# The first conditioning product of a two-layer streaming encoder, taken in two halves of its columns

## The chip, the cores and the metric

The kernel runs on one core of a Trainium2 chip. Five engines of that core matter here: TensorE (PE) for matmuls and transposes, VectorE (DVE) and ScalarE (ACT) for elementwise work and for emptying PSUM, GpSimd (POOL) for a few small things, and SyncE (SP), whose queue issues every DMA of this kernel. Each engine runs its own instruction queue in order; semaphores tie them together. The metric is the device time of one execution in microseconds (us). Before the change the median of three runs is 2450.26 us (2447.16 to 2452.15).

## What is computed

The reference is one step of a two-layer encoder over 1024 prompt tokens and 32 sample tokens with 1024 features. Layer 0 is an mLSTM (a chunked matrix-memory mixer with four heads), layer 1 a band attention, and each is followed by a squared-ReLU MLP. What matters for the change is how the first layer's input is made:

```python
def ada_mod(c, w, b):
    return jax.nn.silu(c) @ w + b

sh1, sc1, g1, sh2, sc2, g2 = jnp.split(ada_mod(c, p['w_ada'][l], p['b_ada'][l])[:, None, :], 6, axis=-1)
u = x * (1 + sc1) + sh1
proj = u @ w_in                      # queries and keys, values v, output gate, input and forget gates
```

The vector c is one per sequence (prompt and sample). Shift sh1 and scale sc1 of layer 0 are the first two of six column blocks of w_ada, each 1024 wide: 1024 x 2048 numbers in float32, 8 MB. Nothing of layer 0 can start on u before them. All is float32, and the results must agree with the reference to float32 accuracy, so the large products are made of a high and a low part: each weight and each u is split in two float32r numbers, and three matmuls (high x high, high x low, low x high) make one.

## The kernel before, in words

Features lie on the 128 partitions in eight chunks (KC = 8); tokens are the free dimension, in three blocks TBS of 384, 384 and 288 (the last holds 256 prompt and the 32 sample tokens). A block of 384 is three tiles of 128 tokens.

The start runs like this. `ada_load(k)` fetches the first 2048 columns of w_ada for the 128 rows of chunk k as two loads of 512 KB into a tile `rada` of 8 KB per partition. These tiles come from the ring with the tag `wc`, six buffers that they share with split weights (`w_v`, `w_qk`) and with the rows of the second token block. `ada_mm(k)` multiplies silu(c) (in `cs`) with them, four matmuls of 512 columns into four groups of 32 partitions of one PSUM bank, added up over k. `ada_first` copies the bank to SBUF, transposes it in four pieces and adds the bias `pt2`; the result `ada` holds shift and scale with features on partitions.

Meanwhile `x_load` brings rows of x, and `x_transpose` turns each chunk over on TensorE (three transposes into a bank `xps`, one copy into `xt` by ACT or DVE). `u_chunks` makes u from `xt` and `ada`, chunk by chunk, as a high part (`modulate`: one ACT instruction) and a low part (two DVE instructions by way of `utmp`). `v_weight` loads half of the weights of the values of head 0 (`raw_v`, with 8 columns for the gates) and splits it (ACT makes the high part, DVE the low): w_v_0 covers the chunks 0 to 3, w_v_1 the chunks 4 to 7.

`v_first` then walks over the blocks: for each chunk k, for each token tile of the block, three matmuls of 264 columns (`v_chunk`), and after each chunk it calls `next_u`, which transposes x and makes u of the next block. In all 3 blocks, 9 token tiles, 8 chunks and 3 products are 216 matmuls. Then come the xsp stores of xt, the gate rows (`gate_rows`: transposes `gt`, then rows `ig`, `fr`, and scans on four partitions that end in the transposes `ae_ps`), queries and keys of the heads (`qk_proj`, weights `raw_qk` and `w_qk`), the mLSTM, the output gate, and from some 440 us on the MLP and layer 1. The conditioning for the other blocks of w_ada is made on DVE as filler work, from loads into `ada_room`.

The order in which instructions stand in each engine's queue isn't that of the source alone: a scheduler places them after a time model of its own, and it also decides which DMA stands where in SP's queue. A change at one place thus moves instructions behind it. `flow` is a list of generators that are advanced by `tick` from the main loops; at the start it holds only `small_params` (small loads of parameters).

## Time and profile before

| what | value |
|---|---|
| median of three runs | 2450.26 us |
| the profiled execution | 2451.64 us |
| its span, first to last instruction | 2449.7 us |
| TensorE busy, share of the span | 2386.9 us, 97% |
| VectorE busy | 1919.8 us, 78% |
| ScalarE busy | 1090.7 us, 45% |
| bytes moved, mean rate | 335.15 MB, 137 GB/s |
| mean granted TensorE clock | 0.993 |

Times in a profile row are microseconds from the start of the span. A row of the timeline has the start, the time taken, the engine (PEld is TensorE loading weights, SPq is SyncE's queue issuing DMAs), the line of the kernel, the operation, output and inputs by the program's names, the shape, the count, and in brackets how long the engine had been idle and what ended that. In a row of stretches the first two numbers are the stretch and its length; then comes the busy time and the count for each engine, the granted TensorE clock, the mean busy share of the 16 DMA engines (just above 1 where transfers overlap) and GB/s. A float32 matmul counts as two instructions there in the conditioning.

### The profile page before, as it was taken

How to read it: one execution, taken by the hardware profiler on the slowest of the kernel's cores; microseconds unless marked ns; L12 is line 12 of the kernel's file. 1: busy time of each engine (PE TensorE's matmuls, PEld its weight loads, DVE VectorE, ACT ScalarE, POOL GpSimd, SP SyncE). 2: the span in 40 equal slices, each digit the busy share in tenths (PEclk: the TensorE clock that was granted, in tenths of full speed). 3: DMA queues.
4: the chain of work that ended last, by engine and by line, in shares of the span. 5: the costliest groups of instructions: out<-in, count | busy, mean ns of one | idle time of the engine just before them, and what ended most of it. 6: DMA issues, size and time to landing. Idle time of an engine off the chain costs nothing.

```text
span 2449.7 us, 42910 instructions
## 1 busy us (share of the span) xinstructions
PE 2386.9 (97%) x16580; PEld 2294.7 (94%) x16580; DVE 1919.8 (78%) x4340; ACT 1090.7 (45%) x2264; POOL 167.3 (7%) x315
## 2 busy tenths in 40 slices
PE   7999999999999999999999999999999999899997
PEld 4999999999999999999999977789999999899997
DVE  4899998788678678687488666755998888887878
ACT  4554456283212212212157466763776777222212
POOL 0211100000000000000000224420000000000003
PEclk9999999999999999999999999999999999999999
DMA  7432223412233233233223230041486779966642
GB/s 287 137 102 88 89 80 109 157 35 87 89 101 121 87 104 113 82 116 107 89 77 101 64 73 2 10 117 42 159 275 233 255 256 335 376 234 230 228 156 72
DMA packets 251503, 335.15 MB, mean 137 GB/s; under 512 B 12824, under 2 KB 201644, under 8 KB 250276
## 3 DMA queue, kind: packets, MB, share of 16 engines
q1 hardware_dynamic: 251300, 332.42, 41.4%
q8 instruction: 130, 2.13, 0.4%
q14 instruction: 73, 0.60, 0.1%
HBM read 255.50 MB, written 79.24 MB: 137 GB/s over the span
## 4 chain that ended last, share of the span: by engine, by line
PE 76%; DVE 12%; DMA 4%; ACT 3%; issue 2%; POOL 0%; SPq 0%; ACTq 0%; DVEq 0%; POOLq 0%
PE dn L1409 11%; PE up L1300 6%; PE up L118 6%; PE up L120 6%; PE up L119 6%; PE dn L119 5%; PE dn L118 5%; PE dn L120 5%; PE pv L1749 3%; PE s L1692 2%; PE pt L1727 2%; PE o L118 1%; PE o L119 1%; PE o L120 1%; DMA hd<-HL 1%
## 5 line engine op out<-in xcount | busy, mean ns | idle before, releaser
L1409 PE MATMUL dn<-fx,wf_d 128*128 128x264 f32 x2016 | 254.2, 285 | 6.9 <-DVE ACX L986 3.3
L1409 PEld LDWEIGHTS dn<-fx,wf_d 128*128 128x128 f32 x2016 | 248.7, 188 | 9.3 <-issue 2.9
L119 PE MATMUL dn<-h,w_dn 128*128 128x384 f32 (+1 forms) x768 | 249.5, 325 | 0.0
L118 PE MATMUL up<-U,w_up 128*128 128x384 f32 (+1 forms) x768 | 249.2, 324 | 0.0
L119 PE MATMUL up<-U,w_up 128*128 128x384 f32 (+1 forms) x768 | 247.9, 323 | 0.0
L118 PE MATMUL dn<-h,w_dn 128*128 128x384 f32 (+1 forms) x768 | 247.8, 323 | 0.0
L120 PE MATMUL up<-U,w_up 128*128 128x384 f32 (+1 forms) x768 | 247.6, 322 | 0.0
L120 PE MATMUL dn<-h,w_dn 128*128 128x384 f32 (+1 forms) x768 | 247.3, 322 | 0.0
L986 DVE SCALAR_TENSOR_TENSOR ACX<-dn,ada,ACX 128x264 f32<-128x264 f32 (+5 forms) x400 | 160.1, 426 | 52.6 <-PE dn L1409 39.6
L238 DVE SCALAR_TENSOR_TENSOR aacc<-rada,cs,aacc 128x256 f32<-128x256 f32 x448 | 190.1, 476 | 0.0
L986 DVE SCALAR_TENSOR_TENSOR acc<-dn,ada,acc 128x384 f32<-128x384 f32 (+2 forms) x256 | 119.2, 485 | 47.0 <-PE dn L120 45.6
L1025 ACT ACTIVATE r<-up 128x384 f32<-128x384 f32 (+1 forms) x96 | 44.3, 463 | 243.3 <-PE up L120 236.9
L119 PEld LDWEIGHTS dn<-h,w_dn 128*128 128x128 f32 x768 | 144.5, 188 | 0.2 <-DVE h L1028 0.2
L120 PEld LDWEIGHTS dn<-h,w_dn 128*128 128x128 f32 x768 | 144.5, 188 | 0.0
L120 PEld LDWEIGHTS up<-U,w_up 128*128 128x128 f32 x768 | 144.3, 188 | 0.0
L118 PEld LDWEIGHTS up<-U,w_up 128*128 128x128 f32 x768 | 144.2, 188 | 0.1
L119 PEld LDWEIGHTS up<-U,w_up 128*128 128x128 f32 x768 | 144.2, 188 | 0.0
L118 PEld LDWEIGHTS dn<-h,w_dn 128*128 128x128 f32 x768 | 143.9, 187 | 0.2
L1300 PE MATMUL up<-u,wf_u 128*128 128x264 f32 x1056 | 139.6, 284 | 1.3 <-ACT wf_u L89 0.6
L1300 PEld LDWEIGHTS up<-u,wf_u 128*128 128x128 f32 x1056 | 132.6, 188 | 1.9 <-ACT wf_u L89 0.8
L1027 DVE TENSOR_TENSOR r<-r 128x384 f32<-128x384 f32 (+1 forms) x96 | 49.9, 522 | 103.3 <-ACT h L1026 102.9
L89 ACT CAST w_up<-raw_up 128x1024 fp32r<-128x1024 f32 x52 | 54.3, 1046 | 136.4 <-DMA raw_up<-in_w_up_dram 102.5
(386 smaller groups left out, 6575.0 us busy)
## 6 DMA issues: line engine op xcount, KB each, us to landing
rada<-in_w_ada_dram SPq DMA_DIRECT2D x64, 512.0 KB
hd<-HL SPq DMA_DIRECT2D x28, 1056.0 KB
raw_up<-in_w_up_dram SPq DMA_DIRECT2D x52, 512.0 KB
fx<-hd SPq DMA_DIRECT2D x50, 528.0 KB
hd<-HM SPq DMA_DIRECT2D x28, 792.0 KB
raw_dn<-in_w_down_dram SPq DMA_DIRECT2D x36, 512.0 KB
ada_room<-in_w_ada_dram SPq DMA_DIRECT2D x32, 512.0 KB
rdn_u<-in_w_up_dram SPq DMA_DIRECT2D x32, 512.0 KB
```

The lines of the kernel that those rows point to most:

```text
L89: nc.scalar.copy(dst_h, src)
L118: nc.tensor.matmul(ps, wh, mov(0, k), start=(k == 0), stop=False)
L119: nc.tensor.matmul(ps, wh, mov(1, k), start=False, stop=False)
L120: nc.tensor.matmul(ps, wl, mov(0, k), start=False, stop=(k == nk - 1))
L238: nc.vector.scalar_tensor_tensor(acc[:, cnd], raw[:, k], sc, acc[:, cnd], op0=ALU.mult, op1=ALU.add)
L986: nc.vector.scalar_tensor_tensor(xs, ps[:, off + o:off + o + mm_], gate[:, fc, cnd:cnd + 1], xs, op0=ALU.mult, op1=ALU.add)
L1027: nc.vector.tensor_mul(r, r, r)
L1300: nc.tensor.matmul(p, self.ws[w][:, wl, k], moving(f, tp, xl, k), start=first and k + n_ == 0, stop=k == 3 and n_ == 2, skip_group_check=n ...
L1409: nc.tensor.matmul(p, ws[w][:, wl, k], t[:, s0, xl], start=first and k + n_ == 0, stop=k == kg - 1 and n_ == 2, skip_group_check=not first)
L1692: nc.tensor.matmul(s[:, b, :w], qst, kk[i][:, g, k0 + j0:k0 + j0 + w], start=(i == 0), stop=(i == 1))
L1727: nc.tensor.transpose(pt[:kp, j - j0, pr * P:(pr + 1) * P], ps_[pr][:, j * P:j * P + kp], ident)
L1749: nc.tensor.matmul(pv[64 * e:64 * e + 64, :nq], V[:kp, vt0 + j, g * 64:(g + 1) * 64], pts[e][:kp, j, :nq], start=(j == 0), stop=(j == nt - 1))
```

## The change

The 2048 columns are no longer loaded and multiplied at once. The columns of shift and of scale are each cut in two halves of 512, and half hf of both makes u's chunks 4 hf to 4 hf + 3. `ada_load(hf, j)` loads, for two row chunks, 512 columns of the shift and 512 of the scale: again two loads of 512 KB per tile, now with two rows of 2 KB where there was one of 4 KB. `ada_mm(hf, k)` has four matmuls of 256 columns, `ada_first(hf)` works on half of the bank, with copies of 128 columns shared by DVE and ACT, two transposes and two bias additions, into a bank of its own.

The order in the source: the first half's four tiles at the start, then x of block 0, `ada_mm(0, ...)`, w_v_0, the loads of the second half, `ada_first(0)`, the transposes of x, w_v_1, the loads of x for the next blocks, and four chunks of u. `v_first` then begins; after its fourth chunk `next_u` runs the second half (`ada_mm(1, ...)`, `ada_first(1)`), the other four chunks of u and the small loads, and the x and u work for block 1 is done two chunks at a time over the last four chunks of block 0.

What the scheduler made of it is seen in the queues. In the rows below, `rada_1_2` is row-chunk pair 2 of half 1; `v_0` to `v_2` are the PSUM banks of the first three token tiles; the number at a name's end only tells buffers apart. TensorE before, from the conditioning's last weights to the first values:

```order
L383 MATMUL ada_139<-rada_5_155,cs 32x512 x4
L383 MATMUL ada_139<-rada_6_180,cs 32x512 x4
L383 MATMUL ada_139<-rada_7_183,cs 32x512 x4
L394 MATMUL adat<-ident,sada 128x128 x4
L366 MATMUL xps_0_313<-ident,xr_0_248 128x128
L366 MATMUL xps_1_331<-ident,xr_0_248 128x128
L435 MATMUL v_0_301<-w_v_0_177,U 128x264
L436 MATMUL v_0_301<-w_v_0_177,U 128x264
```

The same place in the changed kernel, with the last three of the 36 matmuls on w_v_0:

```order
L439 MATMUL v_2_286<-w_v_0_187,U 128x264
L440 MATMUL v_2_286<-w_v_0_187,U 128x264
L441 MATMUL v_2_286<-w_v_0_187,U 128x264
L385 MATMUL ada_139<-rada_1_0_190,cs 32x256 x8
L385 MATMUL ada_139<-rada_1_1_193,cs 32x256 x8
L385 MATMUL ada_139<-rada_1_2_196,cs 32x256 x8
L385 MATMUL ada_139<-rada_1_3_199,cs 32x256 x8
L396 MATMUL adat_356<-ident,sada_355 128x128 x2
L368 MATMUL xps_0_388<-ident,xr_0_256 128x128
L368 MATMUL xps_1_397<-ident,xr_0_256 128x128
L439 MATMUL v_0_284<-w_v_1_253,U 128x264
```

The values of block 0 stood behind the whole conditioning; now their first four chunks, all on w_v_0, stand ahead of its second half, and what follows it works on w_v_1. SP's queue before, behind the small loads (`xsp` is the store of xt, three blocks of tokens; `raw_qk` the weights of queries and keys of heads 0 and 1):

```order
L289 DMA m_92<-in_state_m_dram 4x1
L726 DMA xsp_77<-xt 1024x1x384 x2
L96 DMA raw_qk_0_811<-in_w_in_a_dram 128x4x128 x2
L96 DMA raw_qk_1_817<-in_w_in_a_dram 128x4x128 x2
L96 DMA raw_qk_0_1077<-in_w_in_a_dram 128x4x128
L726 DMA xsp_77<-xt 1024x1x288
L231 DMA ada_room<-in_w_ada_dram 128x4x256
L96 DMA raw_qk_0_1077<-in_w_in_a_dram 128x4x128
```

And now:

```order
L291 DMA m_92<-in_state_m_dram 4x1
L737 DMA xsp_77<-xt 1024x1x384 x2
L737 DMA xsp_77<-xt 1024x1x288
L96 DMA raw_qk_0_850<-in_w_in_a_dram 128x4x128 x2
L96 DMA raw_qk_1_856<-in_w_in_a_dram 128x4x128 x2
L96 DMA raw_qk_0_1116<-in_w_in_a_dram 128x4x128 x2
L96 DMA raw_qk_1_1122<-in_w_in_a_dram 128x4x128
L233 DMA ada_room<-in_w_ada_dram 128x4x256
```

The third store passed five loads of raw_qk, and the first load of the filler conditioning went behind two more of them. At the start of the same queue the order is now: eight loads of the first half, three of x, four of raw_v, eight of the second half; before, four loads of w_ada stood between x and raw_v and four behind raw_v. VectorE before, around the scans of the gate rows (`tt`, `mr`, `rc_rows`, `stk`):

```order
L90 TENSOR_TENSOR w_qk_1_1086<-raw_qk_1_1083,w_qk_1_1086 128x1024
L238 SCALAR_TENSOR_TENSOR ada_room<-ada_room,cs 128x256 x8
L90 TENSOR_TENSOR w_v_0_1448<-raw_v_0_1446,w_v_0_1448 128x1024
L410 SCALAR_TENSOR_TENSOR tt<-fr,tt 4x1056
L245 STREAM_TRANSPOSE ada_room<-ada_room 128x512
L493 SCALAR_TENSOR_TENSOR mr<-tt,ig 4x1024
```

And now:

```order
L243 TENSOR_SCALAR ada_room<-ada_room,cs 128x256 x2
L240 SCALAR_TENSOR_TENSOR ada_room<-ada_room,cs 128x256 x6
L90 TENSOR_TENSOR w_qk_1_1125<-raw_qk_1_1122,w_qk_1_1125 128x1024
L414 SCALAR_TENSOR_TENSOR tt<-fr,tt 4x1056
L90 TENSOR_TENSOR w_v_0_1487<-raw_v_0_1485,w_v_0_1487 128x1024
L497 SCALAR_TENSOR_TENSOR mr<-tt,ig 4x1024
```

Here the filler has done its first eight steps before the scans, where it had done sixteen and their transposition; the low part of a value weight went from ahead of the gate's first VectorE row to behind it. Small moves of this kind go on through the heads of the mLSTM. The diff:

```diff
--- before.py
+++ after.py
@@ -190,11 +190,13 @@
     def wc_tile(shape, name):
         return ring.tile(shape, F32, tag="wc", name=name, bufs=6)
 
-    def ada_load(k):
-
-        raw = wc_tile([P, 2 * D], f"rada_0_{k}")
+    def ada_load(hf, j):
+
+        raw = wc_tile([P, 2, 2, 512], f"rada_0_{hf}_{j}")
         for i in range(2):
-            nc.sync.dma_start(raw[:, i * D:(i + 1) * D], a["w_ada"][0, k * P:(k + 1) * P, i * D:(i + 1) * D])
+            k = 2 * j + i
+            nc.sync.dma_start(raw[:, i], a["w_ada"][0, k * P:(k + 1) * P, :2 * D].rearrange(
+                "p (r h c) -> p h r c", r=2, h=2)[:, hf])
         return raw
     c_rows = raw_tile([16, P], "c_rows")
     nc.sync.dma_start(c_rows[0:8], a["c_prompt"].rearrange("b (k p) -> (b k) p", p=P))
@@ -202,7 +204,7 @@
     rows2 = raw_tile([NPT2, P], "rows2")
     nc.sync.dma_start(rows2[0:96], a["b_ada"].rearrange("l (k p) -> (l k) p", p=P))
     nc.sync.dma_start(rows2[96:112], a["b_ada_kv"].rearrange("(k p) -> k p", p=P))
-    adaw = [ada_load(k) for k in range(4)]
+    adaw = [[ada_load(0, j) for j in range(4)]]
     tp = tpt("tp_c")
     nc.tensor.transpose(tp[:, :16], c_rows, ident[:16, :16])
     cx = cp.tile([P, 4, 16], F32, name="cx")
@@ -377,25 +379,27 @@
 
     ada_ps = adat("ada_0")
 
-    def ada_mm(k):
+    def ada_mm(hf, k):
 
         for q in range(4):
-            nc.tensor.matmul(ada_ps[32 * q:32 * q + 32, :512], cs[:, k, :], adaw[k][:, q * 512:(q + 1) * 512],
+            nc.tensor.matmul(ada_ps[32 * q:32 * q + 32, 256 * hf:256 * hf + 256], cs[:, k, :],
+                             adaw[hf][k // 2][:, k % 2, q // 2, q % 2 * 256:q % 2 * 256 + 256],
                              start=(k == 0), stop=(k == KC - 1))
 
-    def ada_first():
-
-        sb = rc_tile([P, 512], "sada")
-        ps2 = nmt("adat")
-        for hf in range(2):
-            (nc.scalar.copy if hf else nc.vector.tensor_copy)(sb[:, 256 * hf:256 * hf + 256],
-                                                              ada_ps[:, 256 * hf:256 * hf + 256])
-            for b in (2 * hf, 2 * hf + 1):
-                nc.tensor.transpose(ps2[:, b * P:(b + 1) * P], sb[:, b * P:(b + 1) * P], ident)
-        nc.vector.tensor_tensor(
-            ada[:, 0:16, :].rearrange("p (q b) j -> p q b j", q=4),
-            ps2.rearrange("p (b q j) -> p q b j", b=4, q=4)[:, :, :, 0:2],
-            pt2[:, 0:16].rearrange("p (q b) -> p q b", q=4)[:, :, :, None].broadcast_to([P, 4, 4, 2]), op=ALU.add)
+    def ada_first(hf):
+
+        sb = rc_tile([P, 256], f"sada{hf}") if hf else y_tile([P, 256], "sada0")
+        ps2 = nmt(f"adat{hf}")
+        for b in range(2):
+            cols = slice(b * P, (b + 1) * P)
+            (nc.scalar.copy if b else nc.vector.tensor_copy)(sb[:, cols], ada_ps[:, 256 * hf + b * P:256 * hf + b * P + P])
+            nc.tensor.transpose(ps2[:, cols], sb[:, cols], ident)
+        for r in range(2):
+            c0 = r * KC + 4 * hf
+            nc.vector.tensor_tensor(
+                ada[:, c0:c0 + 4, :].rearrange("p (q b) j -> p q b j", q=2),
+                ps2[:, :256].rearrange("p (b r q j) -> p r q b j", b=2, r=2, q=2)[:, r, :, :, 0:2],
+                pt2[:, c0:c0 + 4].rearrange("p (q b) -> p q b", q=2)[:, :, :, None].broadcast_to([P, 2, 2, 2]), op=ALU.add)
 
 
     GATE = 3.0
@@ -693,33 +697,40 @@
     xT = [x_transpose(t0, n, (nc.scalar.copy, nc.vector.tensor_copy)[:2 - (i > 0)]) for i, (t0, n) in enumerate(TBS)]
     uT = [u_chunks(t0, n) for t0, n in TBS]
     x_load(*TBS[0])
-    adaw += [ada_load(k) for k in (4, 5)]
-    for k in range(4):
-        ada_mm(k)
+    for k in range(KC):
+        ada_mm(0, k)
     vw = [v_weight(0, 0)]
-    adaw += [ada_load(k) for k in (6, 7)]
-    for k in range(4, 6):
-        ada_mm(k)
+    adaw.append([ada_load(1, j) for j in range(4)])
+    ada_first(0)
     for _ in xT[0]:
         pass
-    for k in range(6, 8):
-        ada_mm(k)
     vw.append(v_weight(0, 1))
     x_load(*TBS[1], wc_tile)
     x_load(*TBS[2])
-    ada_first()
-    for _ in uT[0]:
-        pass
-    flow.add(small_params(), SP)
+    for k in range(4):
+        next(uT[0])
 
     def next_u(bi, k):
-        if bi < 2:
-            next(xT[bi + 1])
-            next(uT[bi + 1])
-            if k == KC - 1:
-                for g in (xT[bi + 1], uT[bi + 1]):
-                    for _ in g:
-                        pass
+        if bi == 0:
+            if k == 3:
+                for i in range(KC):
+                    ada_mm(1, i)
+                ada_first(1)
+                for _ in uT[0]:
+                    pass
+                flow.add(small_params(), SP)
+            if k < 4:
+                return
+            for _ in range(2):
+                next(xT[1])
+                next(uT[1])
+        elif bi == 1:
+            next(xT[2])
+            next(uT[2])
+        if bi < 2 and k == KC - 1:
+            for g in (xT[bi + 1], uT[bi + 1]):
+                for _ in g:
+                    pass
         flow.tick()
     vts = [v_first(vw, next_u)]
     for t0, n in TBS:
```

## The prediction

> **What bounds the kernel now.** I read the page first, for the share of each engine and the slices of the span.
>
> ```profile
> span 2449.7 us, 42910 instructions
> PE 2386.9 (97%) x16580; PEld 2294.7 (94%) x16580; DVE 1919.8 (78%) x4340; ACT 1090.7 (45%) x2264; POOL 167.3 (7%) x315
> ...
> PE   7999999999999999999999999999999999899997
> ...
> DMA  7432223412233233233223230041486779966642
> ```
>
> TensorE is busy 97% of the span, and only its first slice of 61 us reads 7. So a microsecond is won at the start, if at all. Next I asked for the busy times of each engine by stretch:
>
> ```profile
> core 0: us, PE busy (x) PEld busy (x) DVE busy (x) ACT busy (x) POOL busy (x), PEclk, DMA share, GB/s
> 0.00:20.00 20.00, 10.99 (x40) 2.28 (x40) 2.28 (x14) 2.62 (x6) 1.19 (x12) 1.00 0.85 325
> 20.00:36.00 16.00, 13.18 (x56) 4.23 (x56) 4.80 (x7) 3.96 (x7) 0.00 (x0) 0.79 1.05 387
> 36.00:37.00 1.00, 0.18 (x2) 0.00 (x0) 0.96 (x3) 0.71 (x2) 0.00 (x0) 1.00 1.03 410
> ...
> 40.00:45.00 5.00, 5.00 (x40) 5.00 (x39) 5.00 (x13) 4.37 (x9) 0.00 (x0) 0.90 0.47 172
> ...
> 65.00:70.00 5.00, 5.00 (x43) 5.00 (x42) 3.35 (x8) 2.79 (x5) 0.00 (x0) 1.00 0.83 234
> ...
> 75.00:80.00 5.00, 3.48 (x21) 3.12 (x20) 1.89 (x3) 4.90 (x8) 0.00 (x0) 1.00 0.69 203
> ```
>
> Until 36 us the DMA engines are full (share 0.85, then 1.05) and TensorE has little to do: 96 matmuls in 36 us, against 43 in the 5 us from 65. From 40 on it is full and the DMA is not. So the first 36 us go by bytes, the next 35 by matmuls. The timeline shows where the one hands over to the other:
>
> ```profile
> 32.93 0.19 PEld L383 LDWEIGHTS ada<-rada,cs 128*32 128x32 f32 x4 [1.09 <-DMA rada<-in_w_ada_dram]
> ...
> 34.65 0.42 DVE L391 COPY sada<-ada 128x256 f32<-128x256 f32 x1 [4.32 <-PE ada L383]
> ...
> 36.00 0.19 DVE L395 TENSOR_TENSOR ada<-adat,pt 128x32 f32<-128x32 f32 x1 [0.93 <-PE adat L394]
> ...
> 36.29 4.91 ACT L326 ACTIVATE U<-xt,ada 128x384 fp32r<-128x384 f32 x8 [0.81 <-DVE ada L395]
> ...
> 37.05 0.39 PE L435 MATMUL v<-w_v,U 128*128 128x264 f32 x1 [0.86 <-ACT U L326]
> ...
> 39.18 0.42 PE L436 MATMUL v<-w_v,U 128*128 128x264 f32 x1
> ...
> 39.40 0.42 PE L435 MATMUL v<-w_v,U 128*128 128x264 f32 x1
> ...
> 59.21 0.28 PE L436 MATMUL v<-w_v,U 128*128 128x264 f32 x1
> 59.34 0.28 PE L437 MATMUL v<-w_v,U 128*128 128x264 f32 x1
> ```
>
> The last conditioning weights land at 32.93; their sums are copied, transposed and added to the bias by 36.19; the first value matmul starts at 37.05. At full clock a value matmul follows the last after 0.12 us (59.21 to 59.34, rounded; 0.122 over longer runs), at half clock after 0.22 (39.18 to 39.40). All 216 value matmuls stand behind 37.05.
>
> **The change, part by part.** *36 matmuls move ahead.* The first three token tiles take chunks 0 to 3 of u with w_v_0: 4 chunks x 3 tiles x 3 products = 36. At 0.122 us that is 4.4 us off the stretch after the conditioning, provided that they are done before its second half is in. What they need comes early enough by these rows:
>
> ```profile
> 19.15 0.20 PEld L366 LDWEIGHTS xps<-ident,xr 128*128 128x128 f32 x2 [1.07 <-DMA xr<-in_x_prompt_dram]
> ...
> 26.28 1.07 ACT L89 CAST w_v<-raw_v 128x1056 fp32r<-128x1056 f32 x1
> ...
> 27.97 1.07 ACT L89 CAST w_v<-raw_v 128x1056 fp32r<-128x1056 f32 x1 [0.62 <-DMA raw_v<-in_w_in_a_dram]
> ...
> 29.07 1.26 DVE L90 TENSOR_TENSOR w_v<-raw_v,w_v 128x1056 fp32r<-128x1056 f32 x1 [0.43 <-ACT w_v L89]
> ```
>
> The third row tile of x lands at 19.15 as before, as the same 4 MB stand ahead of it (0.5 us later by the next term). Two tiles of w_ada, four loads of 512 KB at some 1.26 us each (worked out below), no longer stand between it and raw_v, so the first raw_v is in near 21.5 instead of about 26, and its two halves (1.07 of ACT, then 1.26 of DVE, with x copies between) are ready near 24.6. The 36 matmuls then take 4.4 us at full clock and 7.9 at half: done between 29 and 32.5, and the second half of the conditioning is in at 34. So the cover is 1.5 to 5 us thick. If it went, the overhang would come off the 4.4. Behind the burst stand the second half's matmuls on TensorE's queue, and behind those the loads of x for the next tokens, which need their buffers: the first can be issued at 29 to 33 while the queue is still busy until 34, so I count nothing.
>
> *Shorter rows in the conditioning loads.* A load keeps its 512 KB but reads 256 rows of 2 KB where it read 128 of 4 KB. None of the loads of this stage has 2 KB rows; the nearest are 4 KB rows and the 1 KB rows of raw_v:
>
> ```profile
> core 0: us, PE busy (x), PEclk, DMA share, GB/s
> 16.00:22.00 6.00, 3.72 (x20) 0.88 1.03 416
> 23.40:24.60 1.20, 1.20 (x8) 0.76 1.06 358
> ```
>
> 512 KB take 1.26 us at 416 GB/s and 1.46 at 358. The difference, 0.20, belongs to 384 additional rows; 128 additional rows make 0.07. Sixteen loads: +1.1 us (ends 0 and 16 x 0.20 = 3.3). I take the 1.1, since both neighbours are measured in a full queue. The Trainium skill, "DMA: Bandwidth & Descriptors", section on why small descriptors are slow, puts a fixed overhead of about 3 cycles on a packet of 32-byte beats: 67 cycles for 2 KB twice against 131 for 4 KB, an estimate of +2.3% or 0.5 us instead of 1.1. By that rule the two rows above would differ by about 7%; they differ by 16%, so the row is dearer than the rule.
>
> *The tail of the conditioning.* From the last landing to the copy are 1.72 us (32.93 to 34.65) for matmuls of 512 columns; they now have 256. Half would be -0.86; I take -0.7 (ends 0 and -0.86). One bias addition more stands on the path: +0.2 (0.19 in the row). The rest of the additional work (copies, four transposes, the sums of the first half) lies near 16 to 18 us, when ACT and DVE are idle, and on DMA time.
>
> *The store of the last tokens passes the weights of qk.* On SP's queue the third xsp store now stands ahead of the first five loads of raw_qk. Rows of before for that place:
>
> ```profile
> 64.16 0.40 ACT L367 COPY xt<-xps 128x288 f32<-128x288 f32 x1
> ...
> 64.58 0.52 SPq L726 DMA_DIRECT2D xsp<-xt  x1
> ...
> 65.86 3.50 SPq L96 DMA_DIRECT2D raw_qk<-in_w_in_a_dram  x3
> ...
> 72.82 0.28 PE L437 MATMUL v<-w_v,U 128*128 128x264 f32 x1
> ...
> 74.87 1.05 ACT L89 CAST w_qk<-raw_qk 128x1024 fp32r<-128x1024 f32 x1 [1.37 <-DMA raw_qk<-in_w_in_a_dram]
> ...
> 77.24 0.20 PE L488 MATMUL gt<-ident,g 32*36 32x32 f32 x1 [1.52 <-ACT fr L491]
> ```
>
> The store waits for the last copy of x (64.16) and is out at 64.58; the values end 8.3 us later, at 72.82 + 0.12. A load issued behind it at 65.86 was used at 74.87, 9.0 us later. Now the first pair follows the store after 0.6 us, so the first w_qk can be cast some 8.6 to 9.6 us after the store and the values end 8.3 to 8.8 after it (72 matmuls stand behind the last transposes of x). TensorE then waits 0 to 2 us. But before it also waited there, 1.52 for a gate row, because ACT was held by a cast that waited for its load (74.87). The two waits take the same place: ACT's cast comes first, then the gate rows. I add 0.5 us (ends 0 and 2).
>
> *What I cost at nothing.* The half-clock stretch after the hand-over (0.90 in the row 40 to 45, 0.22 us spacing) follows a stretch of thin work in both kernels; if it went, 14 matmuls x 0.1 = 1.4 us less. The planner's new order behind 100 us has no term; a rival has it.
>
> Sum: -4.4 + 1.1 - 0.7 + 0.2 + 0.5 = -3.3 us. The profiled execution took 2451.64 us (span 2449.7 and 1.9 around it), so 2448.3 for its like; it is 1.4 above the median of the three runs, 2450.26, so against that 2447.0.
>
> **The rivals.**
>
> ```profile
> PE ae_ps L523 <- ACT stk L516: 2.2, 1, 2.2
> ...
> 73.61 2.05 DVE L238 SCALAR_TENSOR_TENSOR ada_room<-ada_room,cs 128x256 f32<-128x256 f32 x5
> ...
> 100.00:150.00 50.00, 49.91 (x335) 48.68 (x335) 48.81 (x122) 34.08 (x92) 12.02 (x24) 0.98 0.18 55
> 150.00:200.00 50.00, 48.71 (x316) 44.63 (x315) 46.17 (x146) 21.68 (x64) 7.26 (x21) 1.00 0.41 125
> ```
>
> *More is won than moves.* Between 100 and 200 us VectorE is busy 95 of 100 us and paces the heads. The filler there, ada_room (0.41 us each, 2.05 for 5), now has its first load behind the store and seven raw_qk loads, and by the first y row of VectorE's order 11 of its steps stand where 18 stood: seven, 2.9 us, come later, and what the heads wait on as much earlier. With the half-clock stretch gone too (1.4): -3.3 - 2.9 - 1.4 = -7.6, 2442.7. Against it: the filler is only deferred, and must be paid where VectorE has room.
>
> *The loads take it back.* If 2 KB rows cost like 1 KB rows, 2.2 us more: -1.1, 2449.2, and the change does nothing that can be told. Speaking against it: 2 KB rows have half the row count.
>
> *Slower: the planner's new order stalls the heads.* The scheduler wrote every queue anew up to about 440 us, with small swaps in TensorE's and VectorE's order. TensorE takes its queue in order, so one instruction put ahead of its input holds everything. Such a wait costs 1.52 (gt) or 2.2 (ae_ps) in these rows, about 1.85. Two more of them undo the gain, and above four it is slower by over 0.2%: five give -3.3 + 9.2 = +5.9, 2456.2. For it: both engines are nearly full there, without slack to catch up. Against it: the swaps are between neighbours, and from early in the first MLP on the order is unchanged.
>
> **How the numbers follow.** 0.2% of 2450, 4.9 us, is about what a measurement of this kernel can tell from no change. Forecast (-3.3, from -7 to 0): 0.50, of which 0.18 beyond -4.9. More won: 0.22, all beyond it. Loads take it back: 0.06, no change. Slower order: 0.22, of which 0.20 beyond +4.9. So faster 0.40, within 0.2% 0.40, slower 0.20. The range 2440 to 2456 takes in the first three and the nearer half of the last; the forecast's own is 2443.3 to 2450.3.
>
> **What would show it.** Right: value matmuls between 24 and 32 us while rada still lands; the last rada near 34; the first value matmul on w_v_1 near 37.6; the values ending near 69.5 instead of 72.9; the wait for ae_ps ending near 95. Wrong: a second half that lands after 36 (rows dearer), a w_qk cast later than 72 (store in the way), or values that end early while the start of the first MLP is no earlier or later (order).

## The result, and the profile after

The changed kernel is slower: 2460.51 us median (2459.25 to 2461.25) beside 2447.99 for the kernel before on the same chip, a ratio of 1.0047 (95% interval 1.0034 to 1.006). Measured again (e14) it took 2459.01, ratio 1.0040 (1.0025 to 1.0055). So 10 to 12 us are lost where 3.3 were forecast to be won. The profiled execution took 2460.68 us, its span 2458.9. The page after, totals and slices:

```profile
span 2458.9 us, 43050 instructions
PE 2388.6 (97%) x16644; PEld 2299.0 (93%) x16644; DVE 1923.8 (78%) x4344; ACT 1088.2 (44%) x2265; POOL 161.1 (7%) x315
...
PE   8999999999999999999999989999999999899997
...
q8 instruction: 131, 2.15, 0.4%
```

The first slice reads 8 where it read 7: the start is better filled. TensorE's busy time grew by 1.7 us and the span by 9.2, so most of the loss is idle time elsewhere. The last row (packets, MB and share of the DMA queue that loads the engines' code) comes up again further down. The stretches of the start, changed kernel:

```profile
core 0: us, PE busy (x) PEld busy (x) DVE busy (x) ACT busy (x) POOL busy (x), PEclk, DMA share, GB/s
20.00:36.00 16.00, 13.85 (x120) 10.00 (x118) 7.99 (x14) 6.27 (x10) 0.00 (x0) 1.00 1.05 371
36.00:37.00 1.00, 0.59 (x6) 0.25 (x3) 0.29 (x1) 0.27 (x1) 0.00 (x0) 1.00 1.00 377
...
40.00:45.00 5.00, 5.00 (x42) 4.65 (x41) 4.42 (x10) 4.03 (x10) 0.00 (x0) 1.00 0.15 37
...
75.00:80.00 5.00, 5.00 (x32) 5.00 (x31) 4.84 (x10) 4.49 (x6) 0.00 (x0) 1.00 0.72 209
```

From 20 to 36 us TensorE does 120 matmuls where it did 56, and from 75 to 80 it is busy for 5.00 us instead of 3.48. The rows of the timeline that answer to the forecast's signs:

```profile
23.78 0.59 PE L439 MATMUL v<-w_v,U 128*128 128x264 f32 x1
...
29.90 0.28 PE L441 MATMUL v<-w_v,U 128*128 128x264 f32 x1
...
35.54 0.16 PEld L385 LDWEIGHTS ada<-rada,cs 128*32 128x32 f32 x8 [1.14 <-DMA rada<-in_w_ada_dram]
...
38.35 0.39 PE L439 MATMUL v<-w_v,U 128*128 128x264 f32 x1 [0.91 <-ACT U L328]
...
68.14 1.05 ACT L89 CAST w_qk<-raw_qk 128x1024 fp32r<-128x1024 f32 x1
68.28 0.28 PE L441 MATMUL v<-w_v,U 128*128 128x264 f32 x1
...
93.72 0.72 PE L527 MATMUL ae_ps<-ident,stk 36*128 36x36 f32 x9 [2.16 <-ACT stk L520]
```

The 36 value matmuls run from 23.78 to 29.90, the last conditioning weights are used at 35.54, the values end at 68.41 (72.94 before), and the wait for the gate's transposes ends at 93.72 (98.56 before). The start does, in the main, what it was said to do.

To see where it is given back, I compare the start of the same matmul (the n-th of its kind) in two traces. The kernel before was profiled a second time for this (e8, 2451.93 us, span 2448.4), since one execution of the same program differs from the next by a few microseconds.

> The kernel before once more, for a second profile of it: how much two executions of one program differ in each stage. If the losses at 131 and 430 us are of the order, this profile has neither and agrees with the first to 0.5 us up to 1290 us; the differences found behind 1290 us (1.5 to 4 us) are then seen between these two as well. If this profile shows idle time at 430 us, the first one was a lucky execution.

The table gives the start of matmuls around each time, minus that in the second profile of before, in us; a minus is earlier. The times 67 to 2420 are those of the second profile of before: the last values (67), queries and keys (105), the second head's values (142), output projection (427 and 440), first MLP (600), layer 1 (1900 and 2110), near the end.

| kernel | 67 | 105 | 142 | 427 | 440 | 600 | 1900 | 2110 | 2420 |
|---|---|---|---|---|---|---|---|---|---|
| before, first profile | 1.8 | 1.8 | 1.8 | 2.4 | 2.4 | 1.8 | 1.2 | 1.2 | 1.4 |
| after | -2.7 | -3.3 | 1.2 | 2.4 | 7.5 | 6.3 | 7.3 | 10.3 | 10.5 |
| after, second profile (e14) | -3.6 | -4.2 | -1.3 | -0.4 | 4.3 | 3.2 | 2.5 | 6.3 | 6.2 |

Three places stand out in both profiles of the changed kernel, and none in the first of before: 105 to 142 (4.5 and 2.9 us), 427 to 440 (5.1 and 4.7), 1900 to 2110 (3.0 and 3.8).

**First place: the second head's value weights.** VectorE, ScalarE and TensorE of the changed kernel, timeline:

```profile
96.44 1.05 ACT L89 CAST w_v<-raw_v 128x1024 fp32r<-128x1024 f32 x1 [0.94 <-PE qk L120]
...
131.40 1.32 DVE L559 SCALAR_TENSOR_TENSOR y<-qkp,pt,y 128x1059 f32<-128x1059 f32 x1
...
133.35 0.54 DVE L664 TENSOR_SCALAR hn<-num,sm 128x256 f32<-128x256 f32 x1
...
133.93 1.22 DVE L90 TENSOR_TENSOR w_v<-raw_v,w_v 128x1024 fp32r<-128x1024 f32 x1
134.03 0.67 PE L638 MATMUL cu<-vt,kw 128*128 128x257 f32 x2 [2.85 <-DVE hn L664]
```

and of the kernel before, the same cast and the same subtraction:

```profile
101.83 1.05 ACT L89 CAST w_v<-raw_v 128x1024 fp32r<-128x1024 f32 x1 [1.50 <-PE qk L120]
...
116.05 1.21 DVE L90 TENSOR_TENSOR w_v<-raw_v,w_v 128x1024 fp32r<-128x1024 f32 x1
```

The high part of w_v_1 for the second head (the cast) is ready 5.4 us earlier than before, but its low part, the subtraction on line 90, comes 17.9 us later: in the new VectorE order the rows of three convolutions (y, four rows each) stand between the two, where those of one stood before. Without it only w_v_0, and the high part of w_v_1, can be multiplied, for as many token tiles as have a PSUM bank (39 matmuls, three tiles). Then TensorE reaches the state update `cu`, whose wait ends with hn by the row; hn stands behind y rows too, and TensorE waits 2.85 us. (hn is no input of `cu`; what ties the two together is not shown.) Before, other value matmuls filled that time.

**Second place: the output projection.** VectorE, ScalarE and TensorE of the changed kernel:

```profile
431.11 2.46 DVE L240 SCALAR_TENSOR_TENSOR ada_room<-ada_room,cs 128x256 f32<-128x256 f32 x6
433.48 0.82 DVE L90 TENSOR_TENSOR U<-G,U 128x288 fp32r<-128x288 f32 x2
434.34 1.99 ACT L89 CAST w_oa<-raw_oa 128x1024 fp32r<-128x1024 f32 x2 [6.13 <-DVE U L90]
...
435.44 0.52 PE L118 MATMUL op_a<-U,w_oa 128*128 128x384 f32 x1 [3.27 <-ACT w_oa L89]
```

and of the kernel before:

```profile
426.53 2.46 DVE L238 SCALAR_TENSOR_TENSOR ada_room<-ada_room,cs 128x256 f32<-128x256 f32 x6
428.91 1.55 DVE L90 TENSOR_TENSOR U<-G,U 128x288 fp32r<-128x288 f32 x4
430.50 2.00 ACT L89 CAST w_oa<-raw_oa 128x1024 fp32r<-128x1024 f32 x2 [3.68 <-DVE U L90]
...
433.12 3.24 DVE L238 SCALAR_TENSOR_TENSOR ada_room<-ada_room,cs 128x256 f32<-128x256 f32 x8
```

The last split of U (line 90) lets ScalarE cast the next weights w_oa. Before, it ends at 430.46 and eight rows of the filler (3.24 us) follow it at 433.12; after, it ends at 434.30. Filler rows that had been put off at the start now stand ahead of it: from 415 us to the last split VectorE has 20 of them, before 11, and nine rows of 0.41 us are 3.7 of the 3.8 us by which the split is late. TensorE waits 3.27 us for the cast.

**What a wait costs.** Stretches around both places, changed kernel (columns as above):

```profile
130.00:135.00 5.00, 2.15 (x17) 1.88 (x16) 5.00 (x12) 3.27 (x10) 0.44 (x4) 1.00 0.01 2
135.00:140.00 5.00, 5.00 (x27) 4.60 (x26) 5.00 (x15) 4.20 (x11) 0.60 (x2) 0.66 0.38 105
...
430.00:435.00 5.00, 2.17 (x13) 1.84 (x11) 4.83 (x18) 0.66 (x1) 0.00 (x0) 1.00 0.06 9
435.00:440.00 5.00, 4.57 (x17) 4.57 (x18) 5.00 (x9) 1.33 (x2) 0.00 (x0) 0.66 0.99 332
```

and the kernel before:

```profile
130.00:135.00 5.00, 5.00 (x40) 4.79 (x39) 5.00 (x15) 2.37 (x9) 0.89 (x3) 1.00 0.00 2
...
430.00:435.00 5.00, 5.00 (x31) 5.00 (x30) 5.00 (x15) 2.00 (x2) 0.00 (x0) 1.00 0.94 311
```

TensorE was busy for all of both stretches before. After, it is idle for 2.85 and 2.83 us, and in the 5 us that follow its granted clock averages 0.66, which I put at 5 x 0.34 = 1.7 us lost once more, an estimate: 2.85 + 1.7 = 4.55 against the 4.5 of the table, 3.27 + 1.7 = 4.97 against 5.1. In the second profile of the changed kernel (e14) the first wait is as long (TensorE idle 2.84 from 130 to 135) but the clock behind it stays at 1.00, and there the table shows 2.9: the wait alone.

**Third place: layer 1.** From 1900 to 2110 every queue holds the same instructions in the same order as before, so here it is not the order. VectorE waits more often for its weights; the runs on it are told below.

### The profile page after: what moved, and what is told of

The parts are those of the page before. It is cut to its first block, busy times and chain, and to the rows that moved or that the text cites. A ratio compares the mean times of both kernels' runs of the same rounds, so it can differ in the third digit from the quotient of the medians.

```text
span 2458.9 us, 43050 instructions
## 1 busy us (share of the span) xinstructions
PE 2388.6 (97%) x16644; PEld 2299.0 (93%) x16644; DVE 1923.8 (78%) x4344; ACT 1088.2 (44%) x2265; POOL 161.1 (7%) x315
## 3 DMA queue, kind: packets, MB, share of 16 engines
q8 instruction: 131, 2.15, 0.4%
## 4 chain that ended last, share of the span: by engine, by line
PE 76%; DVE 13%; DMA 5%; ACT 3%; issue 2%; POOL 0%; SPq 0%; ACTq 0%; DVEq 0%; POOLq 0%
PE dn L1420 11%; PE up L1311 5%; PE up L118 5%; PE up L120 5%; PE up L119 5%; PE dn L119 5%; PE dn L118 5%; PE dn L120 5%; PE pv L1760 3%; PE s L1703 2%; PE pt L1738 2%; PE v L439 1%; PE v L440 1%; PE v L441 1%; PE op_a L118 1%
```

## Experiments

**Which part of the change, and is it the filler?** e2 keeps the loads and products in halves but puts the values back in their old order in the source: the whole second half, then all of u, then the values.

```diff
-    for k in range(4):
-        next(uT[0])
+    for i in range(KC):
+        ada_mm(1, i)
+    ada_first(1)
+    for _ in uT[0]:
+        pass
+    flow.add(small_params(), SP)
     def next_u(bi, k):
...
+        if bi < 2:
+            next(xT[bi + 1])
+            next(uT[bi + 1])
```

> The changed kernel without its second part: conditioning still loaded and computed in two halves of the columns, but all eight chunks of u wait for both, and the values run as in the kernel before. VectorE's order has the filler 8 to 10 rows behind all the same. By the terms of the prediction the start is +1.1 - 0.7 + 0.2 = +0.6 us against the kernel before. Theory A (backlog): on top of that the stall near 430 us, 5 us, and perhaps the one near 130: 2453 to 2464. Rival (the interleaving of values is what upsets the heads): 2447 to 2451.

e1 starts the filler's loads ahead of raw_qk in the changed kernel, so that the filler isn't behind; e4 does the same to the kernel before; e3 does the reverse to the kernel before, and puts the filler off.

```diff
 # e1 (after) and e4 (before)
-    flow.add(ada_l0())
+    flow.add(ada_l0(), now=True)
 # e3 (before)
-    flow.add(ada_l0())
+    flow.add(ada_l0(), 6.0)
```

> The changed kernel with one edit: the filler's first load (ada_room) is issued ahead of the first raw_qk loads, where the change had put it behind seven of them. VectorE's order then has its filler rows where the kernel before had them, to within 1 row nearly everywhere from the third head on (the changed kernel is 6 to 10 rows behind). Theory A, the filler's backlog: the idle time of TensorE at 430 to 435 us goes, w_oa is cast near 425 instead of 434.3, and at least the 5 us lost there come back: 2446 to 2456, and 2443 to 2447 if the loss at 130 to 135 us has the same cause. Theory B, any rewritten order stalls the heads, whatever the filler: 2457 to 2463, as the changed kernel.

> The kernel before with one edit: the filler task starts six units later, so that VectorE's order has its rows 3 to 9 behind through the heads and 8 behind at the end, as in the changed kernel; the conditioning and the values are untouched. Theory A: the start as before, a stall near 430 to 440 us: 2452 to 2462. Rival (what costs is something of the change itself): 2446 to 2450.

> The kernel before with the edit of the first run (the filler's first load ahead of raw_qk). Theory A: VectorE's order is ahead with the filler by 5 to 9 rows in the heads and equal at the end, so nothing is gained at 430 us: 2446 to 2450. If a lead of the filler is worth as much as its lag costs: 2440 to 2445. Theory B (any new order stalls): 2452 or more.

Measured:

| run | us | ratio (95%) | 67 | 105 | 142 | 427 | 440 | 1900 | 2110 |
|---|---|---|---|---|---|---|---|---|---|
| e1, after, filler first | 2456.19 | 1.0024 (1.0015 to 1.0033) | -0.7 | -0.3 | 0.8 | -0.2 | 4.9 | 4.1 | 5.8 |
| e2, halves, values as before | 2454.6 | 1.0022 (1.0013 to 1.0031) | -2.5 | -4.1 | -3.9 | -3.5 | 2.6 | 1.7 | 5.3 |
| e3, before, filler late | 2454.88 | 1.0017 (1.0007 to 1.0027) | 0.2 | -1.3 | -0.1 | 0.1 | 4.7 | 4.5 | 4.4 |
| e4, before, filler first | 2455.18 | 1.0022 (1.0011 to 1.0032) | 0.8 | -1.5 | -0.9 | 1.2 | 6.2 | 1.9 | 1.6 |

e2 gains about as much at 67 as the whole change: the scheduler itself puts the 36 value matmuls on w_v_0 ahead of the second half's last five row chunks (the first three stand among them), though the source has them behind all eight. So the gain comes from the loads in halves, and the new order of the values in the source adds little or nothing at the start. The first loss comes with it: e2 has no wait there (0.2 us from 105 to 142) and is 4 to 6 us faster than the changed kernel (2454.6 against 2459.01 and 2460.51). It isn't bound to it: e1 keeps that order of the source, moves only the filler, and loses 1.1 us there.

The second loss is in all four, 4.6 to 6.1 us from 427 to 440. That the filler being late does it was my theory, and e3 agrees: without any change at the start, a late filler costs 4.6 us. But e1 and e4, whose filler comes early, lose as much, by another instruction. The view of waits of e1 between 415 and 450 us (engine, line, what it waited for, us in total, times, longest), and in e4 the row is the same word for word:

```profile
PE op_a L120 <- DVE w_oa L90: 3.3, 1, 3.3
```

In e1 the low part of w_oa comes late, in the changed kernel the cast of the next one. So it is not one instruction, and not the filler's lag as such. My reading is that this place has no spare time on VectorE: each of these five newly written orders (with the changed kernel's own) waits about 3 us there, whichever VectorE row it puts late. In the kernel before, second profile, the same view shows how narrow it is:

```profile
PE op_a L118 <- ACT w_oa L89: 0.3, 1, 0.3
```

**Take work off VectorE there.** e5 (on e2), e6 (on the changed kernel) and e7 (on the kernel before) take the last eight chunks of the filler, the MLP's gate, out of the heads, and make them beside the first output projection and MLP.

```diff
-        yield from ada_cols(a["w_ada"][0], 2048, 16, 32, adat, tmp_f, ADA_C, raw_f)
-        ada_fix(0, [(2, "g"), (4, "sc"), (5, "g")])
+        yield from ada_cols(a["w_ada"][0], 2048, 16, 24, adat, tmp_f, ADA_C, raw_f)
+        ada_fix(0, [(2, "g"), (4, "sc")])
...
+    def ada_gate():
+        yield from ada_cols(a["w_ada"][0], 2048 + 24 * P, 40, 8, mm, tmp_t, ADA_B)
+        ada_fix(0, [(5, "g")])
+    norms["gate"] = flow.add(ada_gate(), 4.0)
```

> The kernel of the second run (halves, values written as before) with the last quarter of the filler, the 8 chunks of the MLP's gate, taken out of the attention stage and run beside the first output projection, where VectorE is about 60% busy. Theory C, the hinge: at the end of the stage TensorE waits because VectorE has 8 filler rows ahead of the splits of the projection's second weights; those rows are now elsewhere. The second run was 5.8 us ahead of the kernel before at 427 us and lost 6.1 there: the idle time at 425 to 431 goes and the 5.8 stay, 2443 to 2447. If instead VectorE's total work is the bound to the end of the projection: the wait moves to the first sum after the projection, 2449 to 2455.

> The changed kernel with the same edit. Its order through the heads is untouched, so the 5 us that TensorE loses at 131 to 142 us stay and only the 5.1 at 430 to 436 go: 2453 to 2457. If the two losses are one (the filler's backlog): 2447 to 2451. If the filler's place does not matter: 2460.

> The kernel before with the same edit. It has no idle time at 430 us to lose, so theory C gives it nothing: 2448 to 2451. If the edit helps whatever the conditioning (less work of VectorE in the heads), it gains as much as the others: 2443 to 2446.

| run | us | ratio (95%) | 67 | 105 | 142 | 427 | 440 | 600 | 1900 | 2110 |
|---|---|---|---|---|---|---|---|---|---|---|
| e5, e2 with gate later | 2454.01 | 1.0022 (1.0014 to 1.0031) | -0.9 | -2.5 | -2.3 | -1.9 | -1.9 | 0.8 | 0.2 | 4.8 |
| e6, after with gate later | 2460.72 | 1.0045 (1.003 to 1.0061) | -0.9 | -3.0 | 2.1 | 3.9 | 3.9 | 6.9 | 8.7 | 12.8 |
| e7, before with gate later | 2453.0 | 1.0017 (1.0008 to 1.0026) | -0.2 | -1.6 | -1.6 | -1.9 | -1.9 | 1.6 | 2.2 | 1.8 |

The loss at 427 to 440 is gone in all three (0.0), so with fewer rows on VectorE it doesn't arise. But the moved rows are in the way at the next place. Waits of e5 between 500 and 600 us:

```profile
PE up L118 <- ACT w_up L89: 2.5, 1, 2.5
PE dn L120 <- DVE w_dn L90: 1.1, 1, 1.1
```

2.7 to 3.5 us are lost between 440 and 600, in e7 too, which has nothing else changed. The loss was moved, not removed.

**Take the two late rows off VectorE.** e9 gives the one late subtraction of the first place to GpSimd, in the changed kernel. e11 (on e2) gives the last eight splits of U to GpSimd, e12 (on the changed kernel) both.

```diff
 # e9, e12
-        return wtile(f"v{h}_{half}", srcs, 264 if h == 0 else 256)
+        return wtile(f"v{h}_{half}", srcs, 264 if h == 0 else 256, eng=nc.gpsimd if (h, half) == (1, 1) else None)
 # e11, e12
-            split(uap(0, k, t0, n), uap(1, k, t0, n), G[:, k, t0:t0 + n])
+            split(uap(0, k, t0, n), uap(1, k, t0, n), G[:, k, t0:t0 + n], nc.gpsimd if t0 == TBS[2][0] else None)
```

> The changed kernel with the low part of head 1's second value weights (w_v_1) computed by GpSimd instead of VectorE, whose order has it 37 us behind the cast, at 133.9 us. Theory D, loss at 131 to 142 us: TensorE has run three token tiles on the first half of these weights, holds all their banks, and waits for the second half. Then the 5 us at 131 to 142 go, TensorE stays 5 to 6 us ahead to 427 us, and the hinge at 430 us takes back what VectorE cannot deliver earlier, as in the second run: 2454 to 2457. If that wait comes from the conv rows ahead of hn instead: 2459 to 2462.

> The kernel of the second run (halves, values written as before) with the last eight U splits, which the weights of the projection wait for since they take G's place, computed by GpSimd. Theory C (the hinge): VectorE's filler rows no longer stand between the heads and these weights, the idle time at 425 to 431 us goes, 5 to 6 us: 2447 to 2451. If VectorE's total work bounds the end of the stage, the wait moves behind 440 us: 2453 to 2456.

> The changed kernel with both edits: w_v_1's low part and the last eight U splits on GpSimd. If theories C and D are right and the two losses are the change's whole cost up to 440 us, it is 10 us faster than the changed kernel and a little slower to equal to the kernel before with what is lost late: 2447 to 2452. If the losses return elsewhere: 2455 to 2460.

| run | us | ratio (95%) | 67 | 105 | 142 | 427 | 440 | 600 | 1900 | 2110 |
|---|---|---|---|---|---|---|---|---|---|---|
| e9 | 2455.13 | 1.0025 (1.0016 to 1.0034) | 0.2 | -1.9 | -0.2 | 1.7 | 7.9 | 6.7 | 7.2 | 10.2 |
| e11 | 2453.22 | 1.0016 (1.0008 to 1.0024) | -1.1 | -2.6 | -2.4 | -1.6 | 0.3 | 0.9 | 0.5 | 2.4 |
| e12 | 2453.98 | 1.002 (1.0011 to 1.0029) | -3.5 | -4.1 | -4.0 | -4.8 | -2.5 | -1.4 | -1.2 | 1.9 |

In e9 the subtraction takes longer on its new engine, but comes early, and the wait for hn is gone:

```profile
99.69 3.06 POOL L90 TENSOR_TENSOR w_v<-raw_v,w_v 128x1024 fp32r<-128x1024 f32 x1 [2.29 <-DMA al_d<-al]
```

3.06 us on GpSimd instead of 1.22 on VectorE, done at 102.75 instead of 135.15. The changed kernel becomes 4 to 5 us faster by this one row (2455.13 against 2459.01 and 2460.51), so the first loss hangs on it. Its 1.7 us from 105 to 142 go to another wait, 2.4 us for a y row ahead of the scores S; in e12 that is 0.9 us and the table shows 0.1. (e9's profiled execution, 2460.09 us, is the slowest of its ten; its columns from 427 on are those of that execution.) In e11 and e12 the second place still costs 1.9 and 2.3 us instead of 5 to 6; TensorE now waits for the low part of w_oa (1.4 and 1.8 us in all) and the clock stays at 1.00. With both, the lead of the start survives to 1900 us (-1.2), for the first time. That is in a quick execution, though: e12's profiled one took 2451.81 us, and its eleven went from 2451.72 to 2460.93.

**2 KB rows.** e10 is the kernel before with the conditioning loads cut into rows of 2 KB, and nothing else.

```diff
-        raw = wc_tile([P, 2 * D], f"rada_0_{k}")
+        raw = wc_tile([P, 2, 2, 512], f"rada_0_{k}")
...
-            nc.sync.dma_start(raw[:, i * D:(i + 1) * D], a["w_ada"][0, k * P:(k + 1) * P, i * D:(i + 1) * D])
+            nc.sync.dma_start(raw[:, :, i], a["w_ada"][0, k * P:(k + 1) * P, i * D:(i + 1) * D].rearrange(
+                "p (h c) -> p h c", h=2))
```

> The kernel before with the same 32 loads of w_ada cut into rows of 2 KB instead of 4 KB (the two halves of each row land in two places); every queue keeps its order, nothing else changes. The prediction's term: +1.1 us (0 to 3.3), with the first value matmul of 37.05 at 38.2: 2449 to 2452. All five kernels with the halves lost 2 to 4 us more than the others at 1900 to 2140 us, with the same order of instructions: if the 2 KB rows (2048 more packets) cause that, it shows here as well: 2452 to 2455, if not, 1900 to 2140 us stays within 1 us of the kernel before.

Measured: 2450.82 us, ratio 1.0002 (0.9993 to 1.0011). Stretches of e10 while the conditioning lands:

```profile
16.00:22.00 6.00, 3.47 (x15) 1.86 (x16) 0.56 (x1) 0.65 (x2) 0.00 (x0) 0.87 1.03 402
28.00:34.00 6.00, 3.70 (x12) 0.52 (x12) 2.52 (x2) 1.48 (x2) 0.00 (x0) 0.72 1.05 386
```

and of the kernel before, second profile:

```profile
16.00:22.00 6.00, 3.69 (x17) 1.81 (x13) 0.56 (x1) 0.96 (x2) 0.00 (x0) 0.80 1.03 417
28.00:34.00 6.00, 4.54 (x16) 0.66 (x16) 2.19 (x2) 1.07 (x1) 0.00 (x0) 0.72 1.02 407
```

The rate falls from 417 and 407 to 402 and 386 GB/s (4 and 5%), and every matmul from 67 to 427 us starts 1.1 us later. That is the forecast's term to the tenth, which is partly luck, since the two profiles of before differ by 1.8 us there. It is not the cause of the 10 to 12 us.

**Layer 1: is it the code?** e13 is the kernel before with the conditioning multiplied in halves of its columns, 64 matmuls of 256 columns instead of 32 of 512, but loaded as before and both halves in one place. (Its columns of shift and scale land in other places than the reference's, so its results are of no use; the number and the shapes of its instructions are as described.)

```diff
-            nc.tensor.matmul(ada_ps[32 * q:32 * q + 32, :512], cs[:, k, :], adaw[k][:, q * 512:(q + 1) * 512],
-                             start=(k == 0), stop=(k == KC - 1))
+            for hf in range(2):
+                nc.tensor.matmul(ada_ps[hf][32 * q:32 * q + 32, 0:256], cs[:, k, :],
+                                 adaw[k][:, q * 512 + 256 * hf:q * 512 + 256 * hf + 256],
+                                 start=(k == 0), stop=(k == KC - 1))
...
-    ada_first()
+    ada_first(0)
+    ada_first(1)
```

> The kernel before with the conditioning computed in two halves of its columns on TensorE, ScalarE and VectorE (64 matmuls of 256 columns instead of 32 of 512, two sets of copies and bias additions), but loaded as before, all of it ahead of the values. If the additional instructions cause the loss at 2030 to 2110 us (the instruction stream is longer by 64 rows there): 2 to 3 us are lost between 2030 and 2110. If not (it belongs to when the loads arrive or to the time at which that stage begins): within 1 us of the kernel before there. The whole: 2448 to 2454.

It took 2453.21 us, ratio 1.0011 (1.0002 to 1.0021), and its profile loses nothing at 427 to 440 but 3.4 us from 1900 to 2110, with the order of all queues unchanged there. (It also loses 2.1 us from 105 to 142, 1.1 of them in a wait for a y row.) A float32 matmul of the conditioning counts twice, so both e13 and the changed kernel have 64 more matmuls and 64 more weight loads on TensorE than the kernel before. So I added such instructions alone, at the very start, while TensorE has nothing to do: 64 (e15, a loop of 65) and 128 (e16, a loop of 129) small transposes to the kernel before, and 64 to the changed kernel (e17), which makes 128 in all. e14 is the changed kernel as it is.

```diff
-    nc.tensor.transpose(tp[:, :16], c_rows, ident[:16, :16])
+    for _ in range(65):
+        nc.tensor.transpose(tp[:, :16], c_rows, ident[:16, :16])
```

> The changed kernel once more, unaltered, for a second profile: losses at 131 to 142 us (5 to 6 us), at 430 to 436 (5 us) and at 2030 to 2110 (2 to 3 us) again, if they belong to the program and not to one execution; time 2458 to 2462.

> The kernel before with 64 more transposes of 16 x 128 at the very start, where TensorE is idle; the same rows in the same order behind. Theory E (where the packets of TensorE's code fall in the program): as in the kernels with the halves, 2 to 3.5 us are lost between 1900 and 2110 us, 2451 to 2453. If the third loss belongs to the conditioning itself: nothing lost there, 2448 to 2451.

> The same with 128 more transposes. If 128 matmuls with their weight loads fill one packet of code (16 KB), the packets behind fall where they fell in the kernel before: nothing lost between 1900 and 2110 us, 2448 to 2451. If what counts is only the number of instructions: 2 us or more are lost as well.

> The changed kernel with 64 more transposes at the start, 128 more matmuls than the kernel before in all. Theory E: the losses at 131 and 430 us stay, the one at 2030 to 2110 goes: 2456 to 2458.5. If not, as the changed kernel: 2459 to 2461.

| run | more TensorE pairs | us | ratio (95%) | lost from 1900 to 2110 |
|---|---|---|---|---|
| before, first profile | 0 | 2450.26 | | 0.0 |
| e10, 2 KB rows | 0 | 2450.82 | 1.0002 (0.9993 to 1.0011) | -0.6 |
| e15 | 64 | 2452.38 | 1.0008 (0.9998 to 1.0017) | 4.2 |
| e13 | 64 | 2453.21 | 1.0011 (1.0002 to 1.0021) | 3.4 |
| after; e14 | 64 | 2459.01 (e14) | 1.0040 (1.0025 to 1.0055) | 3.0; 3.8 |
| e16 | 128 | 2450.27 | 0.9998 (0.9988 to 1.0007) | -0.1 |
| e17 | 128 | 2456.54 | 1.0028 (1.0016 to 1.004) | -0.1 |

The loss comes with 64 and is away with 128, in the kernel before and in the changed one. By its whole time alone e15 can't be told from the kernel before (the interval reaches 0.9998), and its profiled execution, like that of e17, is the slowest of its run. But the same line divides all twenty profiles of this document: the nine with 0 or 128 more pairs lose -0.6 to 1.0 us from 1900 to 2110, the eleven with 64 more lose 1.7 to 4.6. The place shows in VectorE's waits for rdn_u, weights of layer 1, from 1850 to 2070 us. Before:

```profile
DVE s_u L1264 <- DMA rdn_u<-in_w_up_dram: 1.5, 2, 1.1
```

After, then e15 (64 more), e16 (128 more) and e17 (after with 64 more):

```profile
DVE s_u L1275 <- DMA rdn_u<-in_w_up_dram: 5.4, 7, 1.4
```
```profile
DVE s_u L1265 <- DMA rdn_u<-in_w_up_dram: 4.8, 6, 1.2
```
```profile
DVE s_u L1265 <- DMA rdn_u<-in_w_up_dram: 1.9, 2, 1.3
```
```profile
DVE s_u L1276 <- DMA rdn_u<-in_w_up_dram: 2.6, 2, 1.3
```

In all twenty profiles it is one to three waits (0.7 to 2.6 us) where the loss is away, five to seven (3.5 to 6.9 us) where it is there. What 64 more pairs change for instructions 2 ms later, and 128 don't, is their position in the code: the code comes in packets of 2.15 MB / 131 = 16.4 KB over a DMA queue of its own (the row of the page shown above). Before, the row is

```profile
q8 instruction: 130, 2.13, 0.4%
```

With 64 and with 128 more pairs alike the row reads 131, so it can't tell them apart, but the packets' own records in the traces can. Each has 16,384 bytes, and in layer 1, between 1880 and 2000 us, 256 TensorE instructions run from one packet to the next on average over all twenty profiles. So 128 more pairs, 256 instructions, are one packet, and 64 are half of one. Put on the second profile of before by the shift of the matmuls around them, packets start at 1850.2 to 1850.3 and at 1865.0 to 1865.6 us in all nine profiles without the loss, e16 and e17 among them, and at 1856.8 to 1857.5, about halfway, in all eleven with it. That the count of TensorE instructions decides, and that it moves the code packets against the loads of rdn_u, is shown; how a packet there delays a load I have not seen in a trace.

**All three together.** e18 is e12 with 64 more transposes: each found loss has its remedy.

> The changed kernel with all three edits: w_v_1's low part and the last eight U splits on GpSimd, and 64 more transposes at the start. The twelfth run, with the first two, took 2453.98 and lost 3.0 us between 1900 and 2110 us in its profile: without that 2451. If the three losses are the whole difference to the forecast: 2446 to 2449, faster than the kernel before. If it stays at 2451 or above, about 2 to 4 us more are lost in places not found.

It took 2452.09 us, ratio 1.0011 (1.0002 to 1.002): 7 to 8 us faster than the changed kernel (2459.01 and 2460.51), still 2.7 us slower than the kernel before (0.0011 x 2449). Its table row is -2.2 at 67, -2.6 at 142, -1.0 at 427, 2.9 at 440, -1.4 at 1900, -0.9 at 2420, for an execution of 2449.24 us, one of the quickest of its eleven. The second place still costs it 3.9 us by a wait of

```profile
PE op_a L120 <- DVE w_oa L90: 2.1, 1, 2.1
```

and half clock behind it (0.69 in the stretch from 430 to 435), which the start's 2 to 3 us don't cover; and 4.3 us come back between 600 (2.9) and 1900, which no edit accounts for. 3.4 of them come back between 1360 and 1460, where the granted clock (mean from 1395 to 1475) is 1.00 in this profile and 0.91 in the second profile of before (0.96 in the first), so this may be luck of the execution. Where the time goes in its slower executions no profile shows, and that stays open. No run is faster than the kernel before by more than its interval.

## Why the prediction was wrong

**The sum of the start held, in part by luck.** By the end of the values the changed kernel is 2.7 us ahead of the second profile of before and 4.5 ahead of the first; the forecast's terms without the store make 3.8. Point by point: the 36 matmuls were done at 30.2 (forecast between 29 and 32.5). The last conditioning weights were used at 35.54, and at 34.68 in e14 (forecast near 34; behind 36 was named as wrong). The first value matmul on w_v_1 came at 38.35, and at 37.49 in e14 (37.6). The values ended at 68.41 (69.5). The gate's wait ended at 93.72 (95). The 2 KB rows cost 1.1 us, as taken, by e10. But two terms missed and cancelled: beside the second profile of before the last weights were used 2.2 us later (1.4 in e14), not 1.1, and from there to the first value matmul took 2.81 us instead of 3.51 (4.12 in the first profile), 0.7 to 1.3 us less where 0.5 were forecast.

**The store's term had the wrong sign.** I added 0.5 us for a cast of w_qk that waits for its load. It ran at 68.14, while the last values were multiplied, and the wait for the gate row (1.52) was gone, which the stretch from 75 to 80 shows: 5.00 us busy, not 3.48. A wait of 0.6 us for the low part of w_qk took part of its place. So about 0.5 to 1 us was won there.

**The half-clock stretch belonged to the execution.** I had said that it follows thin work "in both kernels", and might go. It isn't even in every execution of the kernel before. First profile:

```profile
38.00:40.00 2.00, 2.00 (x11) 2.00 (x10) 2.00 (x5) 2.00 (x5) 0.00 (x0) 0.50 0.79 217
```

Second:

```profile
38.00:40.00 2.00, 2.00 (x19) 2.00 (x18) 2.00 (x6) 2.00 (x4) 0.00 (x0) 1.00 0.72 210
```

8 matmuls more in the same 2 us, and 1.8 us at 67 us between two executions of one program. A gain read against one profile carries that much chance.

**The step that failed** is under "What I cost at nothing": "The planner's new order behind 100 us has no term". It cost 4.5 us (2.9 in e14) between 105 and 142 and 5.1 (4.7) at 427 to 440. The rival "Slower: the planner's new order stalls the heads" had the right mechanism with a chance of 0.22, and the right argument: "both engines are nearly full there, without slack to catch up". Its price was wrong in form. It counted five waits of 1.85 us; there are two of about 3 us, and up to 1.7 us of half clock behind each. "The swaps are between neighbours" was wrong: the subtraction on w_v_1 moved by 18 us. That row was in the changed order, and its consumers could have been followed: cast early, low part late, one weight tile left for TensorE.

**"More is won than moves"** had the answer in its own "against": the filler "must be paid where VectorE has room". I didn't ask where that is. It isn't at 430 us, where the second profile of before already shows a wait of 0.3 us on the last cast. e3 shows it: the filler put off in the kernel before costs 4.6 us there and wins nothing that lasts.

**"From early in the first MLP on the order is unchanged"** is true, and still 3.0 to 3.8 us were lost behind it, from 1900 to 2110, by 64 more TensorE pairs (e15, e16, e17). The change's added instructions were costed only for the time that they take at the start.

In sum, from the second profile of before to the profile of after: -2.7 to 67, -0.6 to 105, +4.5, +1.2 between 142 and 427, +5.1, -1.2 to 600, +1.0 to 1900, +3.0, +0.2: 10.5 us, the difference of the spans (2458.9 - 2448.4). The three losses with a cause make 12.6 of it, 9.6 of them by the order.

## What to carry to other kernels

Where a scheduler writes the queues anew, a gain at the start is safe only if the new order is followed up to the next places without slack: list, in the profile of before, the waits under half a microsecond on a full engine, and look at what now stands ahead of the row that ends each. A late row on VectorE costs TensorE its wait and sometimes half as much again for the clock behind it, so one badly placed subtraction of 1.2 us cost 3 to 4.5 here. And before a difference of 3 us is put down to a change, profile the kernel before twice, and try the same kernel with some idle instructions added.

## What was not expected of the hardware

64 TensorE transposes and their weight loads, put where the engine is idle, cost 4.2 us some 1.9 ms later in one profile (ratio of e15: 1.0008, 0.9998 to 1.0017), and 128 cost nothing there (e16: -0.1; 0.9998, 0.9988 to 1.0007); the same 64 took the loss out of the changed kernel's profile (3.0 and 3.8 us before, -0.1 with them). The change of the clock after a wait is not fixed: after 2.85 us of idle TensorE it averaged 0.66 over the next 5 us in one execution, and 1.00 in another of the same program. The Trainium skill, "TensorE: Matmul & The Clock Gate", Part 1 on the clock gate, has half clock follow after at least one idle window of about 3.4 us; here 2.85 and 3.27 us of waiting were enough in one execution, so the measurement goes below that figure, and where the windows lie no run here shows. And a subtraction of 128 x 1024 takes 3.06 us on GpSimd against 1.22 on VectorE, and moving it there still made the changed kernel 4 to 5 us faster (e9), since VectorE had a queue at that place.
